# Down projection of a decoder block: eight instead of seven of eleven weight tiles with seven products for eight, four of them with sums formed ahead

## The chip, the core and the metric

The kernel is a whole decoder block for 256 tokens on one core of one Trainium2 chip. The core has five engines that run side by side, each through its own queue in order: TensorE (PE) multiplies matrices, VectorE (DVE) and ScalarE (ACT) do element-wise work, GpSimd (POOL) little of it here, and SyncE (SP) issues most of the DMAs. Weights come from the device's memory (HBM) into the on-chip memory (SBUF); products are accumulated in the banks of PSUM. The metric is the device time of one execution in microseconds (us). Before the change it is 488.08 us, the median of three runs (488.03 to 488.14).

## What is computed

All in float32. `x` is 256 x 1024, the feed-forward width is 2816:

```python
proj = jnp.einsum('bsd,dn->bsn', x, w_in)                  # 1024 -> 9216, split into eight parts
y_a = hgrn2_mixer(...)                                     # gated linear recurrence, normed and gated
y_b = moba_attention(q_b, k_b, mv)                         # causal attention, 8 heads of 128
z_a = jnp.einsum('bsc,cd->bsd', y_a, w_branch_a)           # the two branch projections
z_b = jnp.einsum('bsc,cd->bsd', y_b, w_branch_b)
mixed = jnp.einsum('bsc,cd->bsd', g_a * z_a + g_b * z_b, w_out)
x = layer_norm(DN_ALPHA * x + mixed, ln1_w, ln1_b)
h = jnp.einsum('bsd,df->bsf', x, w_ffn_in)                 # 1024 -> 2 x 2816
h_gate, h_up = jnp.split(h, 2, axis=-1)
y = jnp.einsum('bsf,fd->bsd', jax.nn.silu(h_gate) * h_up, w_ffn_down)   # 2816 -> 1024: the down projection
return layer_norm(DN_ALPHA * x + y, ln2_w, ln2_b)
```

## The kernel before

**Split operands.** Every operand of a large product is kept as two parts, a high one (`wh`, `xh`, rounded to the fast format) and a low one (`wl`, the rest), and a product is three matmuls: high by high, high by low, low by high. The high part of a weight tile is one cast on ACT, the low part one subtraction on DVE (`stage`, L221 and L223). So each weight tile of 1 MB passes DMA, ACT and DVE before PE can read it.

**Weight tiles.** `plan()` lists 77 tiles in the order of use: 0 to 31 for the input projection, 32 to 35 and 36 to 39 for the two branch projections, 40 to 43 for the output projection, 44 to 65 for the feed-forward's first product (gate and up of eleven steps, two feature tiles of 128 each), 66 to 76 for the down projection. I call the last eleven D0 to D10. `fetch()` keeps up to three tiles ready ahead of the one that it hands out; raw tiles have 3 buffers, high and low parts 4 each. The list `loads` is what `stage` goes through; a load of kind "ahead" hands out nothing.

**Seven products for eight.** A tile of the down projection holds two feature tiles of 128 by 1024 outputs, and with the 256 tokens it is a product of 2 x 2 blocks by 2 x 2 blocks. A plain tile does its eight block products, 24 matmuls with 512 columns (`rows_pass`, L827 to L829). A tile in `FAST` does seven (`fast`, L1014 to L1016), 21 matmuls, on three blocks of the weights as they are (the "corners") and four sums of blocks, each split into high and low part. On the other side, seven of eight blocks of the activations and their sums are needed: `ffn_step` forms them with four additions of 128 x 128 on DVE (L982 to L985) and splits 7 x 128 columns, where a plain step splits 4 x 128 (`act_plain`, "ap" in the profile, for `act_fast`, "as").

**Kinds.** The string `DOWN` gives each of the eleven tiles a letter. P is plain. S is fast with its weight sums formed in the down projection, by three instructions on DVE from the raw tile (`make_sums`, L235, L237, L238, into a part of `cst` that is free by then and into the tile `sums`); after that come the split of the corners (L257 on ACT, L260 on DVE) and of the sums (L273 and L275, in two halves). T is fast with its sums formed ahead: at an earlier point of `loads` the raw tile is loaded once more, the sums are formed and stored to a scratch tensor in HBM through POOL's queue (L246); later the corners (768 KB) and the stored sums (1 MB, L264) are loaded and split (L266 and L268, one piece). `SUMS_AFTER` says where the T tiles' sums are formed.

**Order.** From the last two feed-forward steps on (`ORDERED = 2`: steps 9 and 10) and in the output projection, PE, DVE and ACT run in the order in which the code is written; everywhere else, and for SP throughout, a scheduler sets the order when the program is built. Each engine's queue is fixed after that: an instruction that waits holds back all that stand behind it. The down projection's products begin when the last feed-forward step's are done.

The two places where the kinds decide what is issued:

```python
n = 1 if i in spilled else 0
nc.sync.dma_start(b[:, n:4, :], view(wts[i])[:, n:4, :])
sums = make_sums(b) if n == 0 else iter(())
```

Of the kernel before, what the change touches and what calls it, by code (L numbers as in the profile page):

```python
# [17 lines left out]
P = 128  # L18
# [6 lines left out]
NF = FF // P  # L25
# [14 lines left out]
SUMS = 2  # L40
ORDERED = 2
LAGS = (0,1,3,5)
DOWN = "SSPSTSTSPPP"
SUMS_AFTER = (8,12)
FAST = tuple(range(2, 2 + len(DOWN) - DOWN.count("P")))
PLAIN = tuple(q for q in range(NF // 2) if q not in FAST)
SEQUENCE = [PLAIN[DOWN[:i].count("P")] if s == "P" else FAST[i - DOWN[:i].count("P")] for i, s in enumerate(DOWN)]
AHEAD = [q for q, s in zip(SEQUENCE, DOWN) if s == "T"]

# [33 lines left out]
def plan():  # L83

    tiles = []

    def add(w, k0, kn, c0, n, held=False):
        tiles.append((w, k0, kn, c0 if isinstance(c0, tuple) else (c0,), n, held))

    def feat(w, c0, n):  # L90
        for c in range(c0, c0 + n, 256):
            add(w, 0, 8, c, 256)

    def tok(w, c0, n):
        for c in range(c0, c0 + n, 512):
            add(w, 0, 4, c, 512)
            add(w, 4, 4, c, 512)

    feat("w_in", 0, 1024)
    tok("w_in", 2048, 1024)  # L100
    tok("w_in", 3072, 1024)
    tok("w_in", 6144, 512)
    tok("w_in", 8192, 1024)
    for c in range(2):
        if c == 1:
            tok("w_in", 6144 + 512, 512)
        for j in range(2 * c, 2 * c + 2):
            feat("w_in", 5120 + j * 256, 256)
            feat("w_in", 4096 + j * 256, 256)
    tok("w_in", 7168, 1024)  # L110
    tok("w_branch_a", 0, 1024)
    tok("w_branch_b", 0, 1024)
    for k in range(0, KC, 2):
        add("w_out", k, 2, 0, 1024)
    for j in range(0, EARLY, 2):
        for k in range(0, KC, 4):
            add("w_ffn_in", k, 4, (j * P, FF + j * P), 256, j < HOLD_IN)
    for j in range(EARLY, NF, 2):
        add("w_ffn_in", 0, 8, j * P, 256)
        add("w_ffn_in", 0, 8, FF + j * P, 256)  # L120
    for q in SEQUENCE:
        add("w_ffn_down", 2 * q, 2, 0, 1024)
    return tiles
# [3 lines left out]
def hybrid_layer_kernel(ctx: ExitStack, tc, x, xw, vecs, bias, wts, ln1_w, ln1_b, ln2_w, ln2_b, consts, out):  # L127
# [47 lines left out]
    loads = []  # L175
    tiles = plan()
    down = {t[1] // 2: i for i, t in enumerate(tiles) if t[0] == "w_ffn_down"}
    up = [t[3][0] // P for t in tiles]
    for i, (w, k0, k, _, _, held) in enumerate(tiles):
        fast = w == "w_ffn_down" and k0 // 2 in FAST  # L180
        loads += [(i, k, held, kind) for kind in (("corners", "sums") if fast else ("plain",))]
        if w == "w_ffn_in" and up[i] - NF in SUMS_AFTER:
            loads.append((down[AHEAD[SUMS_AFTER.index(up[i] - NF)]], 2, False, "ahead"))
    ready = []
    held_down = range(len(tiles) - HOLD_DOWN, len(tiles))
    last_raw = []
# [5 lines left out]
    def split(dst_h, dst_l, src):  # L192
        nc.scalar.copy(dst_h, src)
        nc.vector.tensor_sub(dst_l, src, r32(dst_h))
# [84 lines left out]
    def fetch(ahead=LOOKAHEAD):  # L279
        while state["next"] < len(loads) and len(ready) < 1 + ahead:  # L280
            list(stage())
        return ready.pop(0)
# [583 lines left out]
    def fast_parts(i):  # L866
        if i == 0:
            tiles = [klp.tile([P, H * P], F32R, tag="kl", name="ash"), cp.tile([P, D], F32R, tag="bgr", name="asl")]
        else:
            both = slot(f"as{i}", F32R)  # L870
            tiles = [both[:, 0:1024], both[:, 1024:2048]]
        return [z[:, 0:7 * P].rearrange("p (b t) -> p b t", b=7) for z in tiles]
# [46 lines left out]
    with tc.manual_schedule(engines={ET.PE, ET.DVE, ET.Activation}):  # L919
# [3 lines left out]
        tiles = [(2 * q,) + fetch(0) for q in range(4)]  # L923
# [43 lines left out]
    def ffn_step(j):  # L967
# [17 lines left out]
        nc.vector.tensor_sub(z[:, 7, :], z[:, 3, :], z[:, 5, :])  # L985
        act_fast[q] = fast_parts(FAST.index(q))
        split(*act_fast[q], z[:, 1:8, :])
# [4 lines left out]
    with tc.manual_schedule(engines={ET.PE, ET.DVE, ET.Activation}):  # L992
# [11 lines left out]
        begins.update({id(wd0): PLAIN[0]})  # L1004
        begins.update({id(ps): FAST[0] for ps in shared})

        def fast(q):
            ah, al = act_fast[q]
            for products in [((p1, 0, 0), (p2, 2, 2), (p3, 6, 1)),
                             ((p4, 1, 3), (p5, 3, 0), (p6, 4, 2), (p7, 5, 1))]:  # L1010
                wh, wl = fetch()
                for ps, a, b in products:
                    stop = q == FAST[-1] and (ps in shared or ps is p2)
                    nc.tensor.matmul(ps, ah[:, a, :], wh[:, b, :], start=(q == begins[id(ps)]), stop=False)  # L1014
# [156 lines left out]
```

## Time and profile before

| | before |
|---|---|
| median of three runs | 488.08 us |
| profiled execution, device time | 488.07 us |
| its span, first to last instruction | 486.3 us |
| PE busy | 478.7 us (98%), 2877 matmuls |
| DVE busy | 404.3 us (83%) |
| ACT busy | 292.9 us (60%) |
| POOL busy | 38.8 us (8%) |
| granted clock of TensorE | 0.999 |

The profile is one execution. Its views are a page of totals, lists of waits (engine, line and tile that waited, what released it, total, times, longest), and timelines: start and duration in us, engine, line of the kernel, operation, output and inputs with their shapes, number of instructions, and in brackets the idle time of the engine just before, with what ended it. Names have their buffer numbers left out: `raw`, `wh`, `wl` are a plain weight tile's parts, `rawcorners`, `whcorners`, `wlcorners` and `rawsums`, `whsums`, `wlsums` those of a fast one; `room` is the work tile of a feed-forward step, `fg` and `fu` its gate and up products, `wp` a bank of the down projection. Instructions of one engine overlap at their ends, so what one costs in a full queue is the distance of two starts, not its duration. A matmul that is held up is drawn longer.

### The profile page before, as it was taken

The numbers are of one execution on the slowest core, as the hardware profiler recorded it, in microseconds if no ns is written. First come the engines' busy times: TensorE is split into PE (matmuls) and PEld (weight loads), VectorE is DVE, ScalarE is ACT, GpSimd is POOL, SyncE is SP. The second block draws the span as 40 slices with busy tenths as digits, with TensorE's granted clock in tenths as the row PEclk, the third lists the DMA queues.
The fourth block names the chain that finished last, engine by engine and source line by source line (L and its number), as shares of the span: only waits on it lengthen the run. The fifth ranks groups of instructions, "written<-read, shape, count | busy, mean of one in ns | idle before, by whom it ended". The sixth has DMA issues, their size and how long they took to land.

```text
span 486.3 us, 7267 instructions
## 1 busy us (share of the span) xinstructions
PE 478.7 (98%) x2877; PEld 410.6 (84%) x2877; DVE 404.3 (83%) x519; ACT 292.9 (60%) x404; POOL 38.8 (8%) x46
## 2 busy tenths in 40 slices
PE   8999999999999999999999999999999999999994
PEld 8889888878799888888888888888888888888784
DVE  4979899999858879999576778855897878889996
ACT  6798487454755777864844353444565655476673
POOL 0000000000012532330000000000000000000030
PEclk9999999999999999999999999999999999999999
DMA  8987426645453445448356455257869545257852
GB/s 313 416 308 257 174 92 255 218 160 194 166 174 131 139 164 218 173 159 305 144 190 216 160 189 198 90 214 269 305 223 350 194 173 174 104 221 253 319 143 86
DMA packets 17633, 100.02 MB, mean 206 GB/s; under 512 B 1984, under 2 KB 3776, under 8 KB 7616
## 3 DMA queue, kind: packets, MB, share of 16 engines
q1 hardware_dynamic: 14400, 92.62, 52.5%
q0 software_dynamic: 3056, 6.82, 4.3%
q8 instruction: 22, 0.36, 0.3%
q10 hardware_dynamic: 144, 0.13, 0.1%
q14 instruction: 11, 0.09, 0.0%
HBM read 94.84 MB, written 3.15 MB: 202 GB/s over the span
## 4 chain that ended last, share of the span: by engine, by line
PE 89%; DVE 6%; issue 2%; ACT 1%; DMA 1%; DVEq 0%; POOLq 0%; POOL 0%; SPq 0%
PE fu L336 7%; PE fg L336 7%; PE fg L338 3%; PE fu L338 3%; PE wp L1015 2%; PE wp L1014 2%; PE mk L336 2%; PE mq L336 2%; PE wp L1016 2%; PE hq L336 2%; PE gb L387 2%; PE gb L388 2%; PE hf L361 2%; PE ga L387 2%; PE ga L389 2%
## 5 line engine op out<-in xcount | busy, mean ns | idle before, releaser
L223 DVE TENSOR_TENSOR wl<-raw,wh 128x2048 fp32r<-128x2048 f32 (+1 forms) x71 | 163.4, 2306 | 43.2 <-ACT wh L221 42.8
L221 ACT CAST wh<-raw 128x2048 fp32r<-128x2048 f32 (+1 forms) x71 | 133.6, 1888 | 64.7 <-PE fg L336 14.2
L336 PE MATMUL fg<-x1p,wh 128*128 128x512 f32 x144 | 50.5, 394 | 0.0
L336 PE MATMUL fu<-x1p,wh 128*128 128x512 f32 x144 | 50.4, 394 | 0.0
L338 PE MATMUL fg<-x1p,wl 128*128 128x256 f32 x144 | 40.0, 278 | 0.0
L338 PE MATMUL fu<-x1p,wl 128*128 128x256 f32 x144 | 39.9, 277 | 0.0
L336 PEld LDWEIGHTS fu<-x1p,wh 128*128 128x128 f32 x144 | 27.0, 188 | 6.2
L336 PEld LDWEIGHTS fg<-x1p,wh 128*128 128x128 f32 x144 | 27.0, 188 | 6.1
L338 PEld LDWEIGHTS fg<-x1p,wl 128*128 128x128 f32 x144 | 27.0, 188 | 0.1
L338 PEld LDWEIGHTS fu<-x1p,wl 128*128 128x128 f32 x144 | 27.0, 188 | 0.0
L336 PE MATMUL mq<-xp,wh 128*128 128x512 f32 x48 | 16.8, 395 | 0.0
L336 PE MATMUL mk<-xp,wh 128*128 128x512 f32 x48 | 16.8, 397 | 0.0
L336 PE MATMUL hq<-xp,wh 128*128 128x512 f32 x48 | 16.7, 394 | 0.0
L606 POOL TENSOR_TENSOR ost<-ost,half 128x4 f32<-128x4 f32 x4 | 4.1, 1014 | 147.8 <-DVE ost L605 147.8
L338 PE MATMUL hq<-xp,wl 128*128 128x256 f32 x48 | 13.3, 277 | 0.0
L338 PE MATMUL mk<-xp,wl 128*128 128x256 f32 x48 | 13.2, 282 | 0.0
L338 PE MATMUL mq<-xp,wl 128*128 128x256 f32 x48 | 13.2, 281 | 0.0
L387 PE MATMUL gb<-wh,xp 128*128 128x512 f32 x32 | 12.7, 398 | 0.0
L901 PE MATMUL fe<-wh,x1p 128*128 128x512 f32 x32 | 12.6, 395 | 0.0
L389 PE MATMUL za<-wl,yah 128*128 128x512 f32 x32 | 12.6, 395 | 0.0
L827 PE MATMUL wo<-wh,mTh 128*128 128x512 f32 x32 | 12.6, 394 | 0.0
L387 PE MATMUL ga<-wh,xp 128*128 128x512 f32 x32 | 12.6, 394 | 0.0
(381 smaller groups left out, 1341.4 us busy)
## 6 DMA issues: line engine op xcount, KB each, us to landing
raw<-in_wts_dram SPq DMA_DIRECT2D x69, 1024.0 KB, 4.8
rawcorners<-in_wts_dram SPq DMA_DIRECT2D x5, 1024.0 KB, 4.8
xw<-in_xw_dram SPq DMA_DIRECT2D x6, 640.0 KB, 9.3
rawahead<-in_wts_dram SPq DMA_DIRECT2D x2, 1024.0 KB, 4.9
rawsums<-spill SPq DMA_DIRECT2D x2, 1024.0 KB, 4.8
rawcorners<-in_wts_dram SPq DMA_DIRECT2D x2, 768.0 KB, 5.7
raw<-in_wts_dram SPq DMA_DIRECT2D x2, 512.0 KB, 11.3
xr<-in_x_dram POOLq DMA_DIRECT2D x1, 1024.0 KB, 5.4
```

The source lines that it names most:

```text
L221: nc.scalar.copy(h[:, ks, :], raw[:, ks, :])
L223: eng.tensor_sub(l[:, ks, :], raw[:, ks, :], r32(h[:, ks, :]))
L336: nc.tensor.matmul(ps, wh[:, k, wcol], a.both(k), start=(k == 0), stop=False)
L338: nc.tensor.matmul(ps[:, 0, :], wl[:, k, wcol], a[0, k, slice(0, T)], start=False, stop=(k == KC - 1))
L361: nc.tensor.matmul(ps, wh[:, kk, wcol], xp.both(k), start=False, stop=False)
L387: nc.tensor.matmul(pss[t], ah[:, kk, ts], wh[:, k, :], start=(kk == 0), stop=False)
L388: nc.tensor.matmul(pss[t], al[:, kk, ts], wh[:, k, :], start=False, stop=False)
L389: nc.tensor.matmul(pss[t], ah[:, kk, ts], wl[:, k, :], start=False, stop=(kk == KC - 1))
L827: nc.tensor.matmul(ps, lh(kk)[:, ts], wh[:, k, ns], start=(kk == first), stop=False)
L901: nc.tensor.matmul(ps, x1p[0, kk, ts], wh[:, k, :], start=(kk == 0), stop=False)
L1014: nc.tensor.matmul(ps, ah[:, a, :], wh[:, b, :], start=(q == begins[id(ps)]), stop=False)
L1015: nc.tensor.matmul(ps, ah[:, a, :], wl[:, b, :], start=False, stop=False)
```

## The change

The letters go from `SSPSTSTSPPP` to `TSTSTSTSPPP`. D0 goes from S to T and D2 from plain to T; the other nine keep their letters. There are now eight fast tiles and three plain ones, and four T tiles. Which feature tiles they hold changes too: feed-forward steps 3 to 10 are fast now, where steps 2 to 8 were, so step 2 is plain and steps 9 and 10, the last two, form the sums of their activations. `SUMS_AFTER` now counts weight tiles: the sums of D0 and D2 are formed after tiles 37 and 39 (second branch projection), those of D4 and D6 after tiles 53 and 57, where they were before.

```diff
-DOWN = "SSPSTSTSPPP"
-SUMS_AFTER = (8,12)
-FAST = tuple(range(2, 2 + len(DOWN) - DOWN.count("P")))
+DOWN = "TSTSTSTSPPP"
+SUMS_AFTER = (37, 39, 53, 57)
+FAST = tuple(range(DOWN.count("P"), len(DOWN)))
...
-    up = [t[3][0] // P for t in tiles]
...
-        if w == "w_ffn_in" and up[i] - NF in SUMS_AFTER:
-            loads.append((down[AHEAD[SUMS_AFTER.index(up[i] - NF)]], 2, False, "ahead"))
+        if i in SUMS_AFTER:
+            loads.append((down[AHEAD[SUMS_AFTER.index(i)]], 2, False, "ahead"))
```

The lines after the removed one stand one lower in the changed kernel (L982 is L981 there). Three places show how the queues change.

DVE at the end of the feed-forward, before, from the first up product of step 9 (`fu180`) to the first evacuation of step 10 (`fg200`); 66 is D0:

```order
L974 TENSOR_TENSOR room_3021<-fu180_3781,room_3021 128x256
L194 TENSOR_TENSOR as6_3721<-room_3021,as6_3721 128x896
L974 TENSOR_TENSOR room_3021<-fu181_3798,room_3021 128x256
L977 TENSOR_TENSOR room_3021<-room_3021 128x512
L194 TENSOR_TENSOR ap1_2595<-room_3021,ap1_2595 128x512
L275 TENSOR_TENSOR wlsums66_3823<-cst_89,whsums66_3822 128x1024
L275 TENSOR_TENSOR wlsums66_3823<-sums66_3775,whsums66_3822 128x1024
L974 TENSOR_TENSOR room_3021<-fg200_3828,room_3021 128x256
```

The same place in the changed kernel, with the two rows ahead of it:

```order
L259 TENSOR_TENSOR wlcorners66_3785<-rawcorners66_3786,whcorners66_3784 128x1536
L193 TENSOR_TENSOR as5_3734<-room_3039,as5_3734 128x896
L973 TENSOR_TENSOR room_3039<-fu180_3790,room_3039 128x256
L973 TENSOR_TENSOR room_3039<-fu181_3807,room_3039 128x256
L976 TENSOR_TENSOR room_3039<-room_3039 128x512
L981 TENSOR_TENSOR room_3039<-room_3039 128x128
L982 TENSOR_TENSOR room_3039<-room_3039 128x128
L983 TENSOR_TENSOR room_3039<-room_3039 128x128
L984 TENSOR_TENSOR room_3039<-room_3039 128x128
L193 TENSOR_TENSOR as6_3833<-room_3039,as6_3833 128x896
L267 TENSOR_TENSOR wlsums66_3837<-rawsums66_3838,whsums66_3836 128x2048
L973 TENSOR_TENSOR room_3039<-fg200_3842,room_3039 128x256
```

Step 9's split is wider and has four additions ahead of it, and D0's sums are split in one piece; the three instructions that formed them, which stood between step 9's gate rows, are gone.

ACT in the changed kernel, from step 9's activation cast to the cast of D2's corners (67 is D1, 68 is D2):

```order
L192 CAST as6_3833<-room_3039 128x896
L265 CAST whsums66_3836<-rawsums66_3838 128x2048
L972 COPY room_3039<-fg200_3842 128x256
L972 COPY room_3039<-fg201_3859 128x256
L975 ACTIVATE room_3039<-room_3039 128x512
L256 CAST whcorners67_3881<-rawcorners67_3883 128x1536
L972 COPY room_3039<-fu200_3891 128x256
L972 COPY room_3039<-fu201_3908 128x256
L192 CAST as7_3934<-room_3039 128x896
L272 CAST whsums67_3948<-cst_91 128x1024
L272 CAST whsums67_3948<-sums67_3885 128x1024
L256 CAST whcorners68_3963<-rawcorners68_3965 128x1536
```

The casts of weight sums stand behind the casts of the step's activations, as they did before; the latter are 896 columns now for 512, and D0's sums are one cast of 2048 for two of 1024.

DVE in the branch projections, changed kernel, around the evacuations of the first one (`za`):

```order
L222 TENSOR_TENSOR wl37_2460<-raw37_2458,wh37_2459 128x2048
L236 TENSOR_TENSOR sums66_2490<-rawahead66_2488,cst_91 128x512
L237 TENSOR_TENSOR sums66_2490<-rawahead66_2488,sums66_2490 128x512
L222 TENSOR_TENSOR wl38_2498<-raw38_2496,wh38_2497 128x2048
L193 TENSOR_TENSOR ybl_1435<-po7_2449,ybh_1434 128x256
L783 TENSOR_TENSOR ga_2103<-za1_0_2456,ga_2103 128x512
L783 TENSOR_TENSOR ga_2103<-za1_1_2457,ga_2103 128x512
L234 TENSOR_TENSOR cst_91<-rawahead68_2562 128x1024
L222 TENSOR_TENSOR wl39_2534<-raw39_2532,wh39_2533 128x2048
L236 TENSOR_TENSOR sums68_2564<-rawahead68_2562,cst_91 128x512
L237 TENSOR_TENSOR sums68_2564<-rawahead68_2562,sums68_2564 128x512
L222 TENSOR_TENSOR wl40_2572<-raw40_2570,wh40_2571 128x2048
```

The rows with 66 and 68 are new there; the others stand in the same order as before, but for the split of `ybl`, which now follows one weight tile later.

## The prediction

> **What bounds the kernel now.** I read the page's shares, then PE's waits, then the timelines of PE, DVE and ACT in the down projection. D0 to D10 are its eleven weight tiles in the order of use (66 to 76 in the program's names).
>
> ```profile
> PE 478.7 (98%) x2877; PEld 410.6 (84%) x2877; DVE 404.3 (83%) x519; ACT 292.9 (60%) x404; POOL 38.8 (8%) x46
> PE warm L430 <- PEq L1158: 0.8, 1, 0.8
> PE hf L358 <- ACT fh L193: 0.5, 1, 0.5
> PE sc L557 <- DVE Qt L576: 0.2, 1, 0.2
> ```
>
> By these rows PE is the bound: it waits 1.5 us in all, and three products fewer would be three products gained. But the shares are means over stages. In PE's timeline of the down projection (start, duration) stand:
>
> ```profile
> 454.74 0.39 PE L1014 MATMUL wp<-whcorners,as 128*128 128x512 f32 x1
> ...
> 458.14 0.39 PE L1014 MATMUL wp<-whcorners,as 128*128 128x512 f32 x1
> 458.37 0.43 PE L1015 MATMUL wp<-wlcorners,as 128*128 128x512 f32 x1
> ...
> 460.57 0.50 PE L1015 MATMUL wp<-wlsums,as 128*128 128x512 f32 x1
> ...
> 463.24 0.39 PE L827 MATMUL wp<-wh,ap 128*128 128x512 f32 x1
> ```
>
> From 454.74 to 458.14 there are 15 products, 3.40/15 = 0.227 us each: a fast tile is 21 x 0.227 = 4.76 us, a plain one 24 x 0.227 = 5.44. D7, the last fast tile, takes 463.24 - 458.14 = 5.10, 0.34 more than its work. DVE's timeline says why:
>
> ```profile
> 456.49 1.75 DVE L260 TENSOR_TENSOR wlcorners<-rawcorners,whcorners 128x1536 fp32r<-128x1536 f32 x1
> ...
> 459.30 1.22 DVE L275 TENSOR_TENSOR wlsums<-sums,whsums 128x1024 fp32r<-128x1024 f32 x1
> ```
>
> These end at 458.24 and 460.52; the products that read them start at 458.37 and 460.57. At D7 the weights come from DVE just in time or a little late, which the list of waits doesn't show because a delayed product is drawn longer (0.50 for 0.39). PE and DVE are both the bound there, and what DVE is late at D7 goes to the end.
>
> **PE's side of the change.** D2 becomes fast: three products fewer, 3 x 0.227 = 0.68 us. Had DVE no part in it, the time would be 0.68 shorter.
>
> **DVE's side, first part: up to the sums of D1.** The rows of DVE, before:
>
> ```profile
> 396.45 0.29 DVE L982 TENSOR_TENSOR room<-room 128x128 f32<-128x128 f32 x1
> 396.66 0.28 DVE L984 TENSOR_TENSOR room<-room 128x128 f32<-128x128 f32 x1
> 396.87 0.29 DVE L983 TENSOR_TENSOR room<-room 128x128 f32<-128x128 f32 x1
> 397.19 0.29 DVE L985 TENSOR_TENSOR room<-room 128x128 f32<-128x128 f32 x1
> ...
> 408.42 1.22 DVE L235 TENSOR_TENSOR cst<-rawcorners 128x1024 f32<-128x1024 f32 x1
> ...
> 411.16 1.75 DVE L260 TENSOR_TENSOR wlcorners<-rawcorners,whcorners 128x1536 fp32r<-128x1536 f32 x1
> ...
> 413.16 1.08 DVE L194 TENSOR_TENSOR as<-room,as 128x896 fp32r<-128x896 f32 x1
> ...
> 414.62 0.69 DVE L977 TENSOR_TENSOR room<-room 128x512 f32<-128x512 f32 x1
> 416.00 0.69 DVE L194 TENSOR_TENSOR ap<-room,ap 128x512 fp32r<-128x512 f32 x1 [0.69 <-ACT ap L193]
> 416.94 1.23 DVE L275 TENSOR_TENSOR wlsums<-cst,whsums 128x1024 fp32r<-128x1024 f32 x1 [0.26 <-ACT whsums L273]
> ...
> 419.22 0.75 DVE L974 TENSOR_TENSOR room<-fg,room 128x256 f32<-128x256 f32 x2
> 419.88 1.22 DVE L235 TENSOR_TENSOR cst<-rawcorners 128x1024 f32<-128x1024 f32 x1
> ...
> 424.72 0.42 DVE L974 TENSOR_TENSOR room<-fu,room 128x256 f32<-128x256 f32 x1 [0.16 <-ACT room L973]
> 425.18 0.69 DVE L977 TENSOR_TENSOR room<-room 128x512 f32<-128x512 f32 x1
> 426.56 0.69 DVE L194 TENSOR_TENSOR ap<-room,ap 128x512 fp32r<-128x512 f32 x1 [0.69 <-ACT ap L193]
> 427.51 1.23 DVE L275 TENSOR_TENSOR wlsums<-cst,whsums 128x1024 fp32r<-128x1024 f32 x1 [0.26 <-ACT whsums L273]
> 428.65 1.22 DVE L275 TENSOR_TENSOR wlsums<-sums,whsums 128x1024 fp32r<-128x1024 f32 x1
> 430.27 2.29 DVE L223 TENSOR_TENSOR wl<-raw,wh 128x2048 fp32r<-128x2048 f32 x1 [0.40 <-ACT wh L221]
> 432.48 1.22 DVE L235 TENSOR_TENSOR cst<-rawcorners 128x1024 f32<-128x1024 f32 x1
> ```
>
> And of ACT, for its casts of 896, 1536 and 2048 columns:
>
> ```profile
> 398.54 0.94 ACT L193 CAST as<-room 128x896 fp32r<-128x896 f32 x1
> ...
> 409.08 1.47 ACT L257 CAST whcorners<-rawcorners 128x1536 fp32r<-128x1536 f32 x1
> ...
> 439.35 1.92 ACT L266 CAST whsums<-rawsums 128x2048 fp32r<-128x2048 f32 x1 [1.73 <-PE wp L829]
> ```
>
> I walk the new order of DVE's queue with the start-to-start spacings of these rows. Up to 408.4 both orders are alike, and DVE is in step with PE there.
> - D0's three sums (2.34 us in 408.42 to 411.16) are gone. What stands behind them is D0's corner split, and ACT's cast for it still ends at 409.08 + 1.47 = 410.55: DVE stands idle for 1.7 us, which the sums used to fill. The split ends at 412.24, step 8's activation split (1.00) at 413.24, and gate x up of step 9 starts at 414.08, 0.54 earlier than the 414.62 of before. That is all that the removed 2.34 brings.
> - Step 9 of the feed-forward becomes fast. Where there was a wait of 0.69 for ACT's cast and a split of 0.69, there are four adds of 128x128 (0.32 + 0.21 + 0.21 + 0.29 = 1.03, by the rows at 396.45), ACT's cast of 896 columns (0.94) and a split of 1.00. They run from 414.79 to 417.82; before was done at 416.69.
> - ACT's cast of D0's sums is one piece of 2048 now and stands behind that of the activations: 416.69 to 418.60. DVE waits 0.8, and its split (2.21) ends at 420.83. Before: 419.22, so 1.6 late.
> - The evacuations and D1's sums and corners follow unchanged; gate x up of step 10 starts at 426.53 for 425.18. The swap of step 9 comes again: adds from 427.24, ACT's cast to 429.24, the split to 430.26. D1's two halves (1.13 + 1.22) end at 432.61 for 428.65 + 1.22 = 429.87.
>
> So DVE is 2.74 late there. Work is the smaller part (eight adds 2.06, two larger splits 2 x 0.31, D0's sums -2.34, together +0.3); the rest, 2.4, is waiting for ACT with nothing put in between.
>
> **Second part: D2 to D7.** Before, D2 is one split of 432.48 - 430.27 = 2.21, while PE spends 5.44 on it: there DVE gets ahead, so far that it waits twice (0.40 at 430.27, 0.54 here):
>
> ```profile
> 441.29 2.29 DVE L268 TENSOR_TENSOR wlsums<-rawsums,whsums 128x2048 fp32r<-128x2048 f32 x1 [0.54 <-ACT whsums L266]
> ...
> 450.03 1.75 DVE L260 TENSOR_TENSOR wlcorners<-rawcorners,whcorners 128x1536 fp32r<-128x1536 f32 x1
> 451.70 2.28 DVE L268 TENSOR_TENSOR wlsums<-rawsums,whsums 128x2048 fp32r<-128x2048 f32 x1
> 453.90 1.22 DVE L235 TENSOR_TENSOR cst<-rawcorners 128x1024 f32<-128x1024 f32 x1
> ```
>
> A T tile costs DVE 1.67 + 2.20 = 3.87 (450.03 to 453.90), an S tile 6.53 (453.90 to 459.30, and 1.13). A pair is 10.40 against PE's 9.52: on such pairs DVE loses 0.9 us each and lives on the lead from D2. Now D2 is a T tile: +1.66. The two waits go, with the overlap that each cost (2.29 for a spacing of 2.21): -0.94 - 0.16. D2's second split waits 0.14 for ACT. Sum: +0.70. D7's sums end 2.74 + 0.70 = 3.4 later, at 463.9.
>
> **The end.** PE starts D0 at 424.1 as before (458.14 less six fast tiles and a plain one), wants the second half of D1's sums at 431.15 (31 products later) and stands until 432.61; further waits follow at the S tiles D3, D5, D7, in all 3.4 + 0.68 + the 0.34 of before = 4.4 us. Behind D7 nothing is changed: PE goes on when D7's sums are there, and D10's load takes the buffer of D7's corners, so it moves along. The profiled execution's 488.07 (span 486.3 and 1.8 around it) is 0.01 from the median, 488.08. 488.07 + 3.4 = **491.5 us**.
>
> **What costs nothing.** The two sums that move into the branch projections are 2 x 2.6 us of DVE there:
>
> ```profile
> 240.00:250.00 10.00, 10.00 (x50) 8.37 (x49) 6.78 (x7) 5.48 (x7) 0.00 (x0) 1.00 0.30 105
> 250.00:260.00 10.00, 10.00 (x46) 8.28 (x45) 5.88 (x4) 2.90 (x3) 0.00 (x0) 1.00 0.68 225
> spill<-sums POOLq DMA_DIRECT2D x2, 512.0 KB, 9.6
> ```
>
> DVE (the third busy time) is free in 7.3 of these 20 us, and weights are made up to three tiles ahead, 3 x 5.44 = 16 us of PE. POOL issues four more stores with nothing else to do. The second tile's sums overwrite what the first tile's store reads: 9.6 us, while the two tiles are 2 x 5.44 = 10.9 apart. If the store is late, DVE stands, with the splits of the next tiles and an evacuation queued behind, and eats from those 16 us; only beyond them does it cost. SP issues four more loads, of which the tightest lands 1.2 us ahead of its use in my walk.
>
> Bounds of what no row shows: the adds closer together, and the cast of D0's sums not kept waiting on ACT (0.6 and 1.0 less); every one of the adds at its full duration, and loads that land behind more traffic (0.3 and 1.0 more). 489.9 to 492.8; I take the walk itself, since each of its steps has a row of its own kind.
>
> [...]
>
> **Rivals.**
> - PE decides: DVE catches up and 0.68 is gained, 487.4. For it: 98%, and a list of waits without a DVE split in it. Against: the rows at 458.37 and 460.57. It holds from the point where DVE ends D7's sums by 459.7, where PE would want them (458.14 - 0.68 + 10 x 0.227); my walk is 4.2 later.
> - Only the second part counts: DVE is back in step at D1's sums (429.9), because ACT's casts come early enough to leave no idle time. Then +0.70, 488.8. Against: the adds, cast and split of a step need each other, and DVE's order is fixed.
> - The loads are late as well: the margin of 1.2 is gone and each of the two last S tiles waits 1 us more, 493.5. For it: one more loaded T tile. Against: loads of 1 MB that start when a buffer comes free, as before.
> - The change isn't made as described: the orders show that it is; no chance.
>
> **How the numbers follow.** My forecast 0.80, PE decides 0.06, the second part only 0.09, late loads 0.05. A measurement of this kernel tells 0.2% (1.0 us) from no change. Faster 0.06 (the first rival), same 0.09 (the second), slower 0.85. The range 489.9 to 492.8 holds the forecast with its bounds and leaves the three rivals out, 0.20.
>
> **What would show it.** Right, if DVE's split of D1's sums ends near 432.6 and that of D7's near 463.9, DVE has gaps of about 1.7, 1.0, 0.8 and 1.0 us between 408 and 430 that end with ACT casts, and PE's products of D1, D3, D5 and D7 come late while the first product of D0 keeps its time. Wrong, if D7's sums are there by 461, or if D0 itself starts late, which would put the cost into the branch or feed-forward stage.

## The result, and the profile after

The changed kernel takes 492.19 us (median of 6 runs, 491.85 to 493.59) beside 488.25 of the kernel before (6 runs, 488.03 to 488.50): the ratio is 1.0085, with a 95% interval of 1.0073 to 1.0096, so it is 3.9 us slower. Its profiled execution took 492.14 us with a span of 490.4, against 488.07 and 486.3.

DVE's timeline of the changed kernel, at the places that the prediction walks (start, duration, what it writes, and in brackets the idle time ahead of it):

```profile
410.61 1.76 DVE L259 TENSOR_TENSOR wlcorners<-rawcorners,whcorners 128x1536 fp32r<-128x1536 f32 x1 [1.54 <-ACT whcorners L256]
...
414.85 0.29 DVE L981 TENSOR_TENSOR room<-room 128x128 f32<-128x128 f32 x1
415.18 0.29 DVE L982 TENSOR_TENSOR room<-room 128x128 f32<-128x128 f32 x1
415.39 0.28 DVE L983 TENSOR_TENSOR room<-room 128x128 f32<-128x128 f32 x1
415.59 0.28 DVE L984 TENSOR_TENSOR room<-room 128x128 f32<-128x128 f32 x1
416.88 1.09 DVE L193 TENSOR_TENSOR as<-room,as 128x896 fp32r<-128x896 f32 x1 [1.01 <-ACT as L192]
418.69 2.29 DVE L267 TENSOR_TENSOR wlsums<-rawsums,whsums 128x2048 fp32r<-128x2048 f32 x1 [0.72 <-ACT whsums L265]
...
429.37 1.09 DVE L193 TENSOR_TENSOR as<-room,as 128x896 fp32r<-128x896 f32 x1 [1.01 <-ACT as L192]
...
431.51 1.22 DVE L274 TENSOR_TENSOR wlsums<-sums,whsums 128x1024 fp32r<-128x1024 f32 x1
...
460.08 1.75 DVE L259 TENSOR_TENSOR wlcorners<-rawcorners,whcorners 128x1536 fp32r<-128x1536 f32 x1
...
462.88 1.22 DVE L274 TENSOR_TENSOR wlsums<-sums,whsums 128x1024 fp32r<-128x1024 f32 x1
...
469.14 2.29 DVE L222 TENSOR_TENSOR wl<-raw,wh 128x2048 fp32r<-128x2048 f32 x1 [0.39 <-ACT wh L220]
471.35 0.68 DVE L1020 SCALAR_TENSOR_TENSOR x<-x,wp 128x512 f32<-128x512 f32 x1
...
485.52 1.42 DVE L1078 SCALAR_TENSOR_TENSOR y<-y,n2sum,wb 128x512 f32<-128x512 f32 x2 [0.27 <-POOL n2sum L1131]
```

The four gaps are there: 1.54 us ahead of D0's corner split, 1.01 and 1.01 ahead of the activation splits of steps 9 and 10, 0.72 ahead of the split of D0's sums, each ended by an ACT cast. D1's sums end at 432.73 (431.51 + 1.22), D7's at 464.10: 3.58 later than the 460.52 of before. From D1's sums on the list has no gap on DVE until D9's split (0.16 us).

PE's timeline of the changed kernel, the first product of D0 and the delayed products behind it:

```profile
424.15 0.39 PE L1013 MATMUL wp<-whcorners,ash 128*128 128x512 f32 x1
...
432.78 0.50 PE L1014 MATMUL wp<-wlsums,as 128*128 128x512 f32 x1 [0.99 <-DVE wlsums L274]
...
441.05 0.50 PE L1014 MATMUL wp<-wlcorners,as 128*128 128x512 f32 x1 [0.49 <-DVE wlcorners L259]
...
461.88 0.50 PE L1014 MATMUL wp<-wlcorners,as 128*128 128x512 f32 x1 [0.35 <-DVE wlcorners L259]
...
464.15 0.50 PE L1014 MATMUL wp<-wlsums,as 128*128 128x512 f32 x1
...
483.51 0.28 PE L828 MATMUL more<-wh,ap 128*128 128x256 f32 x1
```

D0 starts when it did (424.12 before), and PE stands at D1 (432.78), D3 (441.05), D7 (461.88, 464.15) and, by a row like that of D7's corners (451.49, with a gap of 0.35), at D5. From 424.15 to 464.15 there are 157 products, 157 x 0.227 = 35.64 us of work: 4.36 us of waiting. The bracketed gaps show half of it (2.18); the rest is drawn into longer records.

What the prediction did not quote of the kernel before is the last stretch of ACT's, DVE's and PE's queues, from their timelines: the cast of D10, what follows D10's split on DVE, the last instructions of PE and DVE, and between these two the step on ACT that reads PE's last product.

```profile
463.40 1.92 ACT L221 CAST wh<-raw 128x2048 fp32r<-128x2048 f32 x1 [0.56 <-PE wp L1016]
...
467.56 0.68 DVE L1021 SCALAR_TENSOR_TENSOR x<-x,wp 128x512 f32<-128x512 f32 x1
...
479.92 0.28 PE L829 MATMUL more<-wh,ap 128*128 128x256 f32 x1
480.24 0.47 ACT L1076 ACTIVATE z<-more,n2sum 128x256 f32<-128x256 f32 x1
...
481.73 1.42 DVE L1079 SCALAR_TENSOR_TENSOR y<-y,n2sum,wb 128x512 f32<-128x512 f32 x2 [0.27 <-POOL n2sum L1132]
```

From the first instruction behind D10's split to DVE's last pass 481.73 - 467.56 = 14.17 us before, and 485.52 - 471.35 = 14.17 after. This stretch is moved as a block, by 3.79 us; PE's last product moves by 3.59. The start of the stretch hangs on D10's cast, which waited before for D7's last product on PE to give its buffer free (463.40). PE's last product ends just before it is wanted, too: it ends at 480.20 before, and ACT reads it from 480.24.

### The profile page after: what moved, and what is told of

It is laid out like the page before. It is cut to its first block, busy times and chain, and to the rows that moved or that the text cites. A ratio compares the mean times of both kernels' runs of the same rounds, so it can differ in the third digit from the quotient of the medians.

```text
span 490.4 us, 7292 instructions
## 1 busy us (share of the span) xinstructions
PE 480.3 (98%) x2874; PEld 410.2 (84%) x2874; DVE 410.0 (84%) x526; ACT 294.3 (60%) x404; POOL 41.0 (8%) x50
## 4 chain that ended last, share of the span: by engine, by line
PE 81%; DVE 10%; issue 3%; ACT 2%; DMA 2%; DVEq 0%; POOLq 0%; POOL 0%; SPq 0%; ACTq 0%
PE fu L335 7%; PE fg L335 7%; PE fg L337 3%; PE fu L337 3%; PE mk L335 2%; PE mq L335 2%; PE hq L335 2%; PE gb L386 2%; PE gb L387 2%; DVE wlcorners L259 2%; PE hf L360 2%; PE ga L386 1%; PE za L386 1%; PE ga L387 1%; PE ga L388 1%
## 5 line engine op out<-in xcount | busy, mean ns | idle before, releaser
L222 DVE TENSOR_TENSOR wl<-raw,wh 128x2048 fp32r<-128x2048 f32 (+1 forms) x70 | 161.1, 2306 | 35.9 <-ACT wh L220 35.4
L220 ACT CAST wh<-raw 128x2048 fp32r<-128x2048 f32 (+1 forms) x70 | 131.7, 1887 | 68.8 <-DMA raw<-in_wts_dram 14.4
L259 DVE TENSOR_TENSOR wlcorners<-rawcorners,whcorners 128x1536 fp32r<-128x1536 f32 x8 | 14.0, 1752 | 1.5 <-ACT whcorners L256 1.5
L256 ACT CAST whcorners<-rawcorners 128x1536 fp32r<-128x1536 f32 x8 | 11.8, 1471 | 2.8 <-DMA rawcorners<-in_wts_dram 2.8
```

Of the source, the lines that this page charges most:

```text
L220: nc.scalar.copy(h[:, ks, :], raw[:, ks, :])
L222: eng.tensor_sub(l[:, ks, :], raw[:, ks, :], r32(h[:, ks, :]))
L256: nc.scalar.copy(h, b[:, 1:4, :])
L259: nc.vector.tensor_sub(l, b[:, 1:4, :], r32(h))
```

## Experiments

Batches of kernels shared runs of the kernel before, with medians of 488.14 to 488.36.

**The branch stage alone.** The kernel before, which forms the sums of D0 and D2 after tiles 37 and 39 as the change does, and stores them where nothing reads them.

```diff
+        if i in (37, 39):
+            loads.append((down[SEQUENCE[0 if i == 37 else 2]], 2, False, "ahead"))
...
+    unread = {down[q]: dram.tile([P, 2048], F32, ...) for q in (SEQUENCE[0], SEQUENCE[2])}
...
-                nc.gpsimd.dma_start(view(spilled[i])[:, 2 * n:2 * n + 2, :], z)
+                nc.gpsimd.dma_start(view((unread if i in unread else spilled)[i])[:, 2 * n:2 * n + 2, :], z)
```

> The kernel before, with nothing but the branch stage's part of the change added: after tiles 37 and 39 the raw tiles of D0 and D2 are loaded once more, their sums formed and stored to a scratch tensor that nobody reads. Theory (the cost is DVE's lateness in the last feed-forward steps and the down projection): no change, 488.2 (within 0.5), and PE starts the first feed-forward product at the same time as before. Rival (the loads, sums and stores of the branch stage hold up the weights there): most of the 3.9 us is here, 490 to 492.

Measured: 488.21 us, ratio 0.9999 (0.9990 to 1.0009). The moved sums cost nothing there that the interval of half a microsecond lets see. The fullest ten-microsecond stretch of that stage in the changed kernel (length, then PE, PEld, DVE, ACT and POOL busy, granted clock, DMA share, GB/s):

```profile
250.00:260.00 10.00, 10.00 (x46) 8.29 (x45) 7.77 (x8) 2.89 (x3) 1.07 (x2) 1.00 0.98 346
```

PE stays at 10.00 of 10 with the DMA engines busy for 0.98 of a stretch (0.68 before).

**D0 alone ahead.** D0 becomes T, D2 stays plain; seven fast tiles in steps 2 to 8, as before.

```diff
-DOWN = "TSTSTSTSPPP"
-SUMS_AFTER = (37, 39, 53, 57)
-FAST = tuple(range(DOWN.count("P"), len(DOWN)))
+DOWN = "TSPSTSTSPPP"
+SUMS_AFTER = (37, 53, 57)
+FAST = tuple(range(2, 2 + len(DOWN) - DOWN.count("P")))
```

> D0 alone goes from S to T (TSPSTSTSPPP, sums formed after tile 37); D2 stays plain and feed-forward steps 2 to 8 stay the fast ones. DVE loses 2.34 us of work between 408 and 411. Theory: what is taken away turns into waiting for ACT's corner cast, and D0's sums come one cast later; DVE is back in step with PE at the last up product (424.7), so D1's sums keep their time (429.9) and the total stays, 488.2 (within 0.4). Rival (DVE's sum of work from 408 on decides): DVE would be 2.3 us early and the 0.34 us that PE stands at D7 would go, 487.9.

Measured: 488.29, 1.0004 (0.9995 to 1.0013). DVE's timeline of this kernel:

```profile
410.74 1.76 DVE L259 TENSOR_TENSOR wlcorners<-rawcorners,whcorners 128x1536 fp32r<-128x1536 f32 x1 [1.54 <-ACT whcorners L256]
...
417.44 2.29 DVE L267 TENSOR_TENSOR wlsums<-rawsums,whsums 128x2048 fp32r<-128x2048 f32 x1 [1.12 <-ACT whsums L265]
...
428.82 1.22 DVE L274 TENSOR_TENSOR wlsums<-sums,whsums 128x1024 fp32r<-128x1024 f32 x1
```

The 2.34 us of sums are gone from this stretch, and D1's sums end at 430.04 for 429.87: the removed work came back as 1.54 and 1.12 us of idle time.

**D2 alone fast.** D0 stays S, D2 becomes T, so that steps 3 to 10 are fast as in the change.

```diff
-DOWN = "TSTSTSTSPPP"
-SUMS_AFTER = (37, 39, 53, 57)
+DOWN = "SSTSTSTSPPP"
+SUMS_AFTER = (39, 53, 57)
```

> D2 alone becomes fast (SSTSTSTSPPP, its sums formed after tile 39), with the fast feed-forward steps 3 to 10 that come with it; D0 stays S. DVE has 2.34 us more work here than in the changed kernel. Theory: that work falls where the changed kernel's DVE waits for ACT, and D0's sums are cast in two halves, a little earlier; D7's sums come 0.2 us earlier than there: 491.9 (491.4 to 492.4). Rival (DVE's sum of work decides): 2.3 above the changed kernel, 494.5.

Measured: 491.37 (491.22 to 491.56), 1.0068 (1.0053 to 1.0083). That is the change's loss but for 0.8 us, and just below the expected range. So D2 with the steps that go with it carries most of the loss. Taking D0's sums off DVE on top of it, as the change does, doesn't help. It may cost a part of the 0.8: all four times here lie below every time of the change, though the two intervals overlap, and counted from D0's first product (423.86 here, 424.15 there) D7's sums end 0.27 us earlier here (463.54 for 464.10), where 0.2 was expected. What makes up the rest is open.

**Step 10 plain.** The change with the fast tiles in steps 2 to 9, so that of the last two steps only step 9 forms sums.

```diff
-FAST = tuple(range(DOWN.count("P"), len(DOWN)))
+FAST = tuple(range(2, 2 + len(DOWN) - DOWN.count("P")))
```

> The changed kernel's letters and sums, but with feed-forward steps 2 to 9 as the fast ones and step 10, the last, plain (the plain tiles at the end hold steps 0, 1 and 10). Only the work behind the last up product changes: no four adds, a cast of 512 columns for 896, a split of 0.69 for 1.00. Theory: DVE ends D1's sums 1.45 us earlier (431.3 for 432.7) and D7's as much earlier, 490.7 (490.3 to 491.1). Rival (the lateness comes from D2's third share alone, steps 9 and 10 are hidden): 492.2. Rival (PE decides once the last step is light): 487.5.

Measured: 490.73, 1.0054 (1.0039 to 1.0069), on the expected value. DVE's timeline has the gaps of a plain step at step 10, 0.69 and 0.26, where the change has 1.01:

```profile
428.38 0.69 DVE L193 TENSOR_TENSOR ap<-room,ap 128x512 fp32r<-128x512 f32 x1 [0.69 <-ACT ap L192]
429.34 1.22 DVE L274 TENSOR_TENSOR wlsums<-cst,whsums 128x1024 fp32r<-128x1024 f32 x1 [0.26 <-ACT whsums L272]
```

**The change once more,** unedited, in the second batch.

> The changed kernel once more, as the measure for the three that run beside it: 492.2 (within 0.4) by every theory.

Measured: 492.16, 1.0079 (1.0063 to 1.0094).

**Work put into the 1.54 us gap.** The change with one more DVE instruction, a maximum over rows of 1024 columns that nothing reads, ahead of the split of D0's corners.

```diff
+    def dose(n):
+        for m in range(n):
+            nc.vector.reduce_max(dosed[:, m:m + 1], x1[:, m, :], axis=mybir.AxisListType.X)
...
+            if i == down[SEQUENCE[0]]:
+                dose(1)
```

> The changed kernel with one instruction more on DVE, a maximum over 1024 columns (1.13 us, result not used), put in front of D0's corner split, where the changed kernel's DVE stands for 1.54 us until ACT's cast is done. Theory: it costs nothing, as after_again (within 0.3). Rival (DVE's sum of work decides): 1.1 us more than after_again.

Measured: 492.03, 1.0077 (1.0060 to 1.0093). DVE's timeline, the split of D0's corners behind the maximum (1.21 us):

```profile
410.31 1.76 DVE L267 TENSOR_TENSOR wlcorners<-rawcorners,whcorners 128x1536 fp32r<-128x1536 f32 x1 [0.42 <-ACT whcorners L262]
```

The gap shrinks from 1.54 to 0.42 and the time stays: more than a microsecond of DVE work is free at this place.

**Without the sums of the S tiles.** The change, with the three instructions that form sums from a tile left out for D1, D3, D5 and D7; their casts and splits read older values, so the sums of these tiles are not computed.

```diff
-            sums = make_sums(b) if n == 0 else iter(())
+            sums = iter(())
+            if n == 0:
+                corners[i] = [cst[:, C_COS:C_COS + D].rearrange("p (b c) -> p b c", b=2)] * 2
```

> The changed kernel without the three instructions that form the weight sums of D1, D3, D5 and D7 (4 x 2.6 us of DVE less; the casts and splits stay and read what lies there, so these four tiles' part of the down projection isn't the reference's). PE's work is unchanged. Theory: DVE keeps ahead of PE from D2 on; only D1's sums still come late, by about 1.1 us behind step 10's activations: 488.5 (488.0 to 489.0). Rival (the loss is on PE, in the branch stage or in late loads of D0's and D2's stored sums): 491 to 492.

Measured: 490.38, 1.0040 (1.0025 to 1.0055). A miss: 1.9 us above what I expected, with about 10 us of work taken off DVE. DVE's timeline, the sum splits of D2, D4 and D6, and ACT's, the cast of D9:

```profile
434.31 2.29 DVE L269 TENSOR_TENSOR wlsums<-rawsums,whsums 128x2048 fp32r<-128x2048 f32 x1
...
444.02 2.29 DVE L269 TENSOR_TENSOR wlsums<-rawsums,whsums 128x2048 fp32r<-128x2048 f32 x1 [1.67 <-ACT whsums L267]
...
454.22 2.29 DVE L269 TENSOR_TENSOR wlsums<-rawsums,whsums 128x2048 fp32r<-128x2048 f32 x1 [1.42 <-ACT whsums L267]
```

```profile
462.10 1.91 ACT L220 CAST wh<-raw 128x2048 fp32r<-128x2048 f32 x1 [2.07 <-DMA raw<-in_wts_dram]
```

A pair of a T and an S tile takes three raw buffers, which is all there are. They go round in 9.71 and 10.20 us, where PE needs 9.52: once DVE is out of the way, ACT waits for loads (1.51 and 1.92 us ahead of its casts of D4's and D6's sums). PE is held for long at D1's sums only (432.65); what the loads cost reaches the end by D10's split, behind which DVE's last stretch begins at 469.56 for 467.56. That reading was formed on this run, and the next one tests it.

**Without the sums, and with less to load.** As the run above; S tiles load three blocks instead of four, and D2, D4 and D6 load half of their stored sums and take the other half from an older tile, so that half of these sums is left out too. The whole cast and split of D2's, D4's and D6's sums become two halves.

```diff
-            nc.sync.dma_start(b[:, n:4, :], view(wts[i])[:, n:4, :])
+            nc.sync.dma_start(b[:, 1:4, :], view(wts[i])[:, 1:4, :])
...
-            nc.sync.dma_start(z, view(spilled[i]))
+            part = i > min(spilled)
+            nc.sync.dma_start(z[:, 0:2, :] if part else z, view(spilled[i])[:, 0:2, :] if part else view(spilled[i]))
...
+            y = cst[:, C_COS:C_COS + D].rearrange("p (b c) -> p b c", b=2)
+            for z, bs in ((z[:, 0:2, :], slice(0, 2)), (y, slice(2, 4))) if part else ((z, slice(0, 4)),):
```

> The kernel without the sums of its S tiles, with less to load besides: S tiles load three blocks (768 KB for 1 MB), and D2, D4 and D6 load half of their stored sums (512 KB for 1 MB) and take the other half from an older tile in memory. Left out are those sums' values; casts, splits and products are as many as before. Theory, formed on the run without the sums (behind DVE the loads through three raw buffers are the next bound: 9.7 to 10.2 us for a pair of T and S): the raw buffers go round in under 9.5 us, PE is held at D1's sums alone (432.65 for 431.15, 1.5 us), and gets back 0.68 and 0.34: 488.07 + 1.5 - 1.0 = 488.6, 488.2 to 489.1. Rival (what held the kernel without sums wasn't the loads but the order of ACT and DVE): 490.4, as there.

Measured: 488.76, 1.0010 (1.0001 to 1.0020). DVE's timeline, the corner splits of D4 and D6:

```profile
440.55 1.76 DVE L261 TENSOR_TENSOR wlcorners<-rawcorners,whcorners 128x1536 fp32r<-128x1536 f32 x1 [0.23 <-ACT whcorners L258]
...
449.16 1.75 DVE L261 TENSOR_TENSOR wlcorners<-rawcorners,whcorners 128x1536 fp32r<-128x1536 f32 x1
```

8.61 us for a pair, and 1.6 us of time came back. Two halves of a cast or split together took no less time than the whole one of the run above: for D2's sums, from start to the next start, 1.89 us for 1.81 on ACT and 2.27 for 2.21 on DVE. But the raw buffer of the stored sums is also free after one half of the cast and split, so the run doesn't part fewer bytes from a buffer that is held for less time. What it shows is that the round through the three raw buffers is the next bound behind DVE. Even this kernel, with neither bound in the second part, is not faster than before: D1's sums still hold PE until 432.50. Behind that no waiting is left: PE takes 47.88 us from there to its last product, and 126 products up to D7's sums with the 19.36 us of the changed kernel behind them (483.51 - 464.15) make 126 x 0.227 + 19.36 = 47.96.

**Work put behind D2's split, in the kernel before.** Two of the same maxima on DVE where it gets its lead.

```diff
+            if i == down[PLAIN[0]]:
+                dose(2)
```

> The kernel before with two maxima over 1024 columns more on DVE (2.26 us, results not used) right behind D2's split, where its DVE gains its lead on PE. Theory: the wait of 0.54 us in front of D4's sums (0.62 with the overlap it costs) takes up a part, the rest arrives at D7 one for one: +1.65, 489.9 (489.5 to 490.3). Rival (PE decides, the lead is ample): 488.2. Rival (every us of DVE counts): 490.5.

Measured: 489.67 (8 runs), 1.0034 (1.0024 to 1.0045). DVE's timeline, the split of D4's sums:

```profile
442.52 2.28 DVE L276 TENSOR_TENSOR wlsums<-rawsums,whsums 128x2048 fp32r<-128x2048 f32 x1
```

Of 2.26 us, 1.5 reach the end; the rest goes into the 0.54 us wait of before, which is gone at 442.52. What DVE loses at D2 is paid once its small reserve of waits is used up.

**The casts of weight sums first.** The change, with the four additions, the cast and the split of steps 9 and 10 moved behind D0's and D1's sums in the order. Nothing is left out or added.

```diff
+            if later:
+                later.pop(0)()
...
-        nc.vector.tensor_add(z[:, 4, :], z[:, 0, :], z[:, 2, :])
...
-        split(*act_fast[q], z[:, 1:8, :])
+        if hold:
+            later.extend((adds, parts))
+        else:
+            adds()
+            parts()
```

> The changed kernel, with the four additions and the activation cast and split of steps 9 and 10 moved in the order: the additions of step 9 behind the split of D0's sums, its cast and split behind step 10's gate evacuations; those of step 10 in the same way behind D1's sums and D2's corners. Nothing is left out, and no instruction is added; what changes is that the weight sums' casts no longer stand behind the activation casts. Theory (of the 2.74 us by which D1's sums are late only 0.3 is work and 2.4 are waits for ACT with nothing put in between): by a walk of the new order with the same rows D1's sums end at about 428.8 instead of 432.7, the activation split of step 10 comes when D1 itself is long running, and D7's sums come 1.5 to 2 us earlier: 490.4, 489.9 to 490.9. Rival (the waits are filled and come back elsewhere, because DVE's work sets the time in this stretch too): 492.2, as the change.

Measured: 490.21 (490.19 to 490.82), 1.0043 (1.0027 to 1.0058). DVE's timeline:

```profile
427.57 1.22 DVE L274 TENSOR_TENSOR wlsums<-sums,whsums 128x1024 fp32r<-128x1024 f32 x1
...
460.93 1.21 DVE L274 TENSOR_TENSOR wlsums<-sums,whsums 128x1024 fp32r<-128x1024 f32 x1
```

The same instructions in another order end D1's sums at 428.79 and D7's at 462.14, and 1.95 us come back. At least that much of the loss was waiting, and the order made it; the additions and splits that were moved back are done behind D1's sums now, so less comes back at D7 than at D1.

**The plain tile third.** Eight fast tiles with four T, as in the change, but D2 stays plain and the fast ones reach to D8, in steps 2 to 9. Meant as a kernel that might beat both.

```diff
-DOWN = "TSTSTSTSPPP"
+DOWN = "TSPTSTSTSPP"
...
-HOLD_DOWN = 3
+HOLD_DOWN = 2
```

> The changed kernel with its plain tile moved: TSPTSTSTSPP, so eight fast tiles as in the change and four of them T, but the third stays plain, and the fast ones hold steps 2 to 9, so that the last step is plain. Theory (the change loses because D2 no longer lets DVE get ahead and because both last steps form sums): D1's sums are no more than 1.5 us late, at D2 DVE gets 3.2 us ahead, and the three pairs of T and S behind it cost 0.9 each: 2.7. D8's sums, the last, end when PE wants them, PE gets its 0.68 and the 0.34 of before: 487.2, 486.9 to 487.9. Second theory, from the run without the sums (three raw buffers go round once in a pair, which took 9.7 and 10.2 us there, against 9.52 of PE): loads and DVE together cost what is gained, 488.2, 487.9 to 488.8. Rival (a fast tile at that place always costs more than it brings): 489 or more.

Measured: 491.45 (490.94 to 491.85), 1.0064 (1.0052 to 1.0077). The largest miss: 4.2 us above the first theory, 3.2 above the second. DVE's timeline (the splits of D9 and D10, which follow on D8's sums, and what comes behind) and PE's (the product that waits for D8's sums, the last one):

```profile
465.76 4.49 DVE L222 TENSOR_TENSOR wl<-raw,wh 128x2048 fp32r<-128x2048 f32 x2
470.16 0.68 DVE L1020 SCALAR_TENSOR_TENSOR x<-x,wp 128x512 f32<-128x512 f32 x1
...
484.32 1.41 DVE L1078 SCALAR_TENSOR_TENSOR y<-y,n2sum,wb 128x512 f32<-128x512 f32 x2 [0.27 <-POOL n2sum L1131]
```

```profile
465.89 0.50 PE L1014 MATMUL wp<-wlsums,as 128*128 128x512 f32 x1
...
479.75 0.28 PE L828 MATMUL more<-wh,ap 128*128 128x256 f32 x1
```

On PE the theory missed by less: D8's sums are there 0.7 us after PE would want them, which leaves little of the 1.0 that it was to gain, and PE's last product stands where it did (479.75, 479.92 before). And yet the kernel ends 3.2 us later (2.9 in the profiled execution). D10's split ends 2.6 us later than before, DVE's last stretch begins 2.6 us later, and its last instruction (484.32) comes 14.16 us behind, for 14.17 before. I had looked at what PE waits for, and not at what DVE still has to do behind D10. That gave a new theory, that DVE and not PE sets the end, with one run to test it.

**Work put behind D10's split, in the kernel before.** The same two maxima at the head of DVE's last stretch.

```diff
+            if i == down[SEQUENCE[-1]]:
+                dose(2)
```

> The kernel before, with two more instructions on DVE (maxima over rows of 1024 columns, 2.26 us in an earlier run) right behind the split of D10, the last weight tile; nothing reads their results, and PE's products of the down projection have all their weights by then. Theory (the end is set by DVE's queue: in the runs so far 14.2 us pass from the end of D10's split to DVE's last instruction, whenever PE ends): +2.2, 490.4, 490.0 to 490.8. Rival (PE's last products set the end, and DVE has room beside them): 488.2 to 488.9.

Measured: 490.40 (490.11 to 491.12) beside 488.36, 1.0047 (1.0030 to 1.0064). DVE's timeline, and PE's last product:

```profile
467.73 2.34 DVE L204 TENSOR_REDUCE dose<-x 128x1 f32<-128x1024 f32 x2
470.18 0.69 DVE L1029 SCALAR_TENSOR_TENSOR x<-x,wp 128x512 f32<-128x512 f32 x1
...
484.35 1.41 DVE L1087 SCALAR_TENSOR_TENSOR y<-y,n2sum,wb 128x512 f32<-128x512 f32 x2 [0.27 <-POOL n2sum L1140]
```

```profile
480.86 0.28 PE L837 MATMUL more<-wh,ap 128*128 128x256 f32 x1
```

All of it reaches the end, as far as the interval tells (+2.0, 1.5 to 3.1), though PE's last product is only 0.94 later. So a delay of DVE's last stretch delays the end of the kernel before, in which PE is busy for 98% of the span. It doesn't follow that PE has room there. The run without the sums and with less to load is the other side; of it, the start and end of DVE's stretch, PE's last product, and the step on ACT that reads it:

```profile
466.35 0.68 DVE L1025 SCALAR_TENSOR_TENSOR x<-x,wp 128x512 f32<-128x512 f32 x1
...
482.12 1.41 DVE L1083 SCALAR_TENSOR_TENSOR y<-y,n2sum,wb 128x512 f32<-128x512 f32 x2 [0.27 <-POOL n2sum L1136]
```

```profile
480.38 0.28 PE L833 MATMUL more<-wh,ap 128*128 128x256 f32 x1
```

```profile
480.70 0.47 ACT L1080 ACTIVATE z<-more,n2sum 128x256 f32<-128x256 f32 x1 [0.39 <-PE more L833]
```

Its stretch begins 1.21 us earlier than before and takes 15.77 us, not the 14.2 that the expectation gives for all runs so far. ACT waits for PE's last product, which is 0.46 later than before, and DVE's last instruction is 0.39 later. Over all runs the last instruction of DVE comes no less than 14.16 us behind the start of the stretch and no less than 1.73 behind PE's last product, and in each run one of the two holds within 0.1 us. In the kernel before both do: 14.17, and 481.73 - 479.92 = 1.81. Two paths end there together. In the changed kernel it is DVE's: 14.17 and 2.01.

## Why the prediction was right, and where its reasons were not

The forecast was 491.5 us and slower; measured were 492.19, within the range and 0.7 above the forecast.

- **DVE up to D1's sums: right.** The walk put their end at 432.61, the trace has 432.73. Its gaps of 1.7, 1.0, 0.8 and 1.0 us are 1.54, 1.01, 0.72 and 1.01. That the removed sums of D0 bring next to nothing was shown from both sides: taken away they leave a gap and no time (D0 alone ahead), and a microsecond of other work fits into the gap for nothing.
- **"The rest, 2.4, is waiting for ACT with nothing put in between": right.** The four gaps of the changed kernel sum to 4.28 us; DVE's gaps of before in the same stretch, by the prediction's rows 0.69, 0.26, 0.16, 0.69 and 0.26, to 2.06. That is 2.2 more, beside the 2.4 of the walk. With the order changed alone, D1's sums came 3.9 us earlier and the end 1.95, as work was moved behind D1's sums.
- **D2 to D7: right.** +0.70 was forecast; from D1's to D7's sums it is 464.10 - 432.73 = 31.37 against 30.65, +0.72. The lead that DVE had from the plain D2 was tested by filling it: 1.5 of 2.26 us reached the end.
- **PE's waits: right.** 4.4 us in all at D1, D3, D5 and D7, and 4.36 by the trace, while D0's first product keeps its time.
- **The branch stage: right.** Nothing, measured by itself.
- **The adds.** With each of the eight adds at its duration of 0.29 us instead of at its spacing, the walk comes to +3.7 (an estimate from the rows: 8 x 0.29 = 2.32 for 2.06, on top of 2.74 + 0.70), nearer to the result than mine. The rows don't bear it out as the reason: the adds at 414.85 to 415.59 start 0.33, 0.21 and 0.20 apart, as before the change, and D1's sums came 0.12 off the walk that used these spacings.
- **"Behind D7 nothing is changed: PE goes on when D7's sums are there, and D10's load takes the buffer of D7's corners, so it moves along": the term that was too small.** The prediction followed PE alone to the end. There is a second path: D10's cast waits for D7's last product and for D10's load, and behind it come D10's split and DVE's stretch of 14.17 us. Before the change both paths end within 0.1 us of each other, and D7's sums delay both, so leaving one out cost little. D7's last product ends 3.6 us later, as D7's sums do, and PE's last product does too; but D10's load now lands so late (467.10) that the cast starts 0.2 behind D7's last product, at 467.20 (chain of waits below). So DVE's last instruction comes 3.79 later and not 3.4: 0.2 of that is the walk up to D7's sums (464.10 for 463.9), 0.2 the load. The 0.2 of the load rests on single executions: in the run with work behind D10's split, alike up to there, that split starts 0.17 later already without the change (465.52 for 465.35), with 0.63 us of waiting for its cast for 0.18. Of the 4.07 us between the two profiled executions 0.3 is left, behind DVE's last instruction; there the kernels of this study spread from 3.0 to 3.5 us, and I can't say by what.
- **"Had DVE no part in it, the time would be 0.68 shorter": it leaves out the raw buffers, which are next in line.** With DVE relieved of about 10 us of sums the kernel still took 490.38. With less to load besides it took 488.76, and there PE's gain does appear: from the second half of D1's sums to its last product PE takes 480.38 - 432.50 = 47.88 us, where it took 479.92 - 431.17 = 48.75 before. That is 0.87 less, of the 0.68 and 0.34 that the prediction counts on for PE, and D1's sums, still late, use it up. No run takes DVE out wholly. The rival with late loads named a resource that the change reaches by 0.2 us at D10, and the kernel without the sums, whose DVE is relieved, by 1.51 and 1.92 us at D4 and D6.
- **The rivals** fall: PE doesn't decide, and D1's sums are far from back in step. That D2's part is not the only one shows in the run with step 10 plain, which gives back 1.4 us.

The chain behind D7's corners, as the view of the chain that ended last has it for the changed kernel (start, duration, engine, what); ahead of these rows stands D7's corner split, behind them D10's split:

```profile
461.86 5.24 DMA raw<-in_wts_dram
467.20 1.92 ACT wh L220
```

The load starts when D7's corner split ends (461.83), as the prediction had it, and ACT waits for it. In that view of the kernel before the last rows go the same way, from D10's cast (463.41) over its split (465.35) and DVE's stretch, with steps on ACT and POOL in between, to DVE's last instructions. The view names one path only; that PE's last product ends just as late stands in the timelines. The prediction rests on the shares of that view, where PE has 89%, and not on its last rows.

## What to carry to other kernels

The products saved on TensorE (0.68 us) were worth nothing here, where another engine prepared their operands just in time and the kernel lost 3.9 us. In such a kernel walk that engine's queue in order, with starts and not durations, and count the waits that a removed instruction leaves behind as well as the work it takes away. Read the last rows of the chain of waits before deciding which engine sets the end; a share of 98% didn't tell. A dose of idle work shows that a delay at its place counts; it doesn't show that another engine has room there, and here two paths ended within 0.1 us. Where the same instructions can stand in another order, put the cast that another engine is about to need ahead of the one that is needed later: that alone was worth half of this loss, 1.95 us.

## What the runs showed of the hardware beyond what I expected

Loads of one size did not take one time. DMA issues from 430 to 480 us of the changed kernel (out and in, queue, count, KB each, median us from issue to landing):

```profile
rawcorners<-in_wts_dram SPq DMA_DIRECT2D x2, 1024.0 KB, 4.7
rawcorners<-in_wts_dram SPq DMA_DIRECT2D x2, 768.0 KB, 4.3
```

The same of the kernel without the S tiles' sums, in which DVE frees raw buffers earlier:

```profile
rawcorners<-in_wts_dram SPq DMA_DIRECT2D x2, 1024.0 KB, 6.5
rawcorners<-in_wts_dram SPq DMA_DIRECT2D x2, 768.0 KB, 5.3
```

These corner loads, two of each size, took 1.0 to 1.8 us longer in the second kernel, while loads of stored sums took 5.6 in both; why is not shown. In the changed kernel a tile with a quarter fewer bytes landed only 0.4 us earlier. I had counted a load as one fixed duration behind a buffer.
